# A fused diffusion layer on one core: which pieces of the first modulation's weights are split, and on which engine

## The chip, the cores and the metric

The kernel runs on one core of a Trainium2 chip. The metric is the device time of one execution in microseconds (us). Below, PE is the tensor engine (matrix products), DVE is VectorE, ACT is ScalarE, POOL is GpSimd and SP is the engine that issues most of the transfers. All data are 32 bit floats.

## What is computed

One layer of a diffusion backbone, on 128 context tokens and 512 latent tokens of width 1024. Two conditioning vectors (one for the context, one for the latent tokens) give shift, scale and gate for both halves of the layer:

```
mod_ctx = silu(c_ctx) @ w_mod + b_mod          # and mod_lat from c
sh1, sc1, gt1, sh2, sc2, gt2 = split(mod, 6)
h = rms_norm(x, gain0) * (1 + sc1) + sh1       # the "first modulation"
y = mixing(h)                                  # w_in, gated DeltaNet scans, short convolution, gates, w_out
x = x + gt1 * rms_norm(y, gain1)
h = rms_norm(x, gain2) * (1 + sc2) + sh2
y = (silu(gate) * up) @ w_ffn_out              # gate, up = split(h @ w_ffn_in, 2)
x = x + gt2 * rms_norm(y, gain3)
```

The mixing part has 8 heads with a chunked recurrent scan in two directions, whose state goes from chunk to chunk, and a short convolution branch `y_b = (bg * conv(cg * xs)) @ w_br_b`.

## The kernel before, in words

**Products in three parts.** A large product is made of three products of a faster number format (fp32r). `split` (L48) makes of a tile a high part, by a cast (L57), and a low part, by subtracting the high part from the tile (L58), each in two instructions of 512 columns: a "pair". By default the cast is on ScalarE and the subtraction on VectorE. `mm3` (L83 to L85) then multiplies high with high, high with low and low with high. `gemm_cm` (L87) does a whole gemm of 8 x 3 products of 320 columns into one PSUM bank `d`; the pool of these has three banks. A bank is free again when its reader has run: ScalarE's tanh L735, or VectorE's multiplications L716 and L724.

**The first modulation** (L762 to L856). Only sh1 and sc1 are needed before the layer's first gemm. Their weights come in two halves (`mods(0)`, `mods(1)`, each 512 of the 1024 channels), in each half for sc1 and sh1 four pieces `mr` of 128 x 2 x 512, so 16 pieces in all, loaded in that order. `mod_mm` (L782) multiplies a piece in one of two ways. A *direct* piece, named in the argument `direct`, goes in as it is, in 32 bit floats (L790, two products). A *split* piece is split first, into `msh` and `msl`, and has four fp32r products (L793 with the high part, L794 with the low part). `lows` and `highs` say on which engine the parts of piece 0, 1, 2, 3 are made: the low part of piece 3 on POOL, the others on VectorE; the high part of piece 2 on VectorE, the others on ScalarE. `mod_end` copies the product to a row `mrow` (L798) and turns it into a column by eight small products L180, copied out by L182. `scale_of` (L249) makes the scale s of sc1. `modulate(h)` then makes four of the eight blocks k of h: on ScalarE the high part hT0 (L811, context and latent columns apart), on VectorE the same in full precision over xT (L813) and the difference as low part hT1 (L815). The gemms of the layer, from L83 on, need these.

**The scans.** For each of four pairs of heads p, `scan(p)` (L599) goes through eight steps. A step has two sub-steps: products L643 with EW, then with KU, each into the PSUM tile s, and after each two copies into the state tile RS, one on ScalarE and one on VectorE (L647 after EW, L658 or L661 after KU). Each sub-step needs the copies of the one before. L673 makes the output products from what is there. Other work is there to fill the gaps: gemms of the gates, `gate_th` (tanh L735 into a tile gt), the short convolution, `short` (L701), and the steps of `row_job` (L185), which adds up the rows of the second modulation on VectorE, two L196 of 128 x 1024 for each weight tile; their sums go through L57/L58 (cph, cpl) and L208/L209 to a row.

**The short convolution.** `short(i)` multiplies two gemms into a tile cx (L710, L716), convolves it into cy (L717, then in `conv` L379, L381 and the two edges L384 and L386, of one column each), and multiplies cy with a third gemm, half by half (L724). cx, cy and the gates' gt take turns in two buffers of one tag, "dt".

**What sets the order.** In the first modulation the order on SP is written out. On the other engines a scheduler of the framework sets the order of all instructions of the program when it is built, from priorities (`high_priority`), the dependences and its own costs. So an edit at one place can change the order elsewhere. An engine runs its instructions in that order.

Of the kernel before, what the change touches and what calls it, by code (L numbers as in the profile page):

```python
# [21 lines left out]
CTX = 128  # L22
LAT = 512
TOK = CTX + LAT
# [13 lines left out]
class Kernel:  # L38
# [700 lines left out]
    def run(self):  # L739
        nc, tc, I, O = self.nc, self.tc, self.I, self.O  # L740
# [21 lines left out]
        with ExitStack() as st:  # L762
            xp = pool(st, "xp")
            psn = pool(st, "psn", 3, space=PSUM)
            psm = pool(st, "psm", 2, space=PSUM)
            ma = lambda: psm.tile([P, 512], F32, name="m", tag="m")
            pri = lambda n: tc.high_priority(offset=n)

            def mod_load(blk, h):
                row = xp.tile([5, 512], F32, name="mrow", tag="mrow", bufs=4)  # L770
                nc.gpsimd.dma_start(out=row[4:5, :], in_=I["b_mod"][blk, :, h * 512:(h + 1) * 512])
                raws = []
                for kk in range(KT // 2):
                    raw = xp.tile([P, 2, 512], F32, name="mr", tag="mr", bufs=9)
                    nc.sync.dma_start(out=raw, in_=I["w_mod1"][blk, h, kk])
                    raws.append(raw)
                return row, raws

            lows = (nc.vector, nc.vector, nc.vector, nc.gpsimd)
            highs = (nc.scalar.copy, nc.scalar.copy, nc.vector.tensor_copy, nc.scalar.copy)  # L780

            def mod_mm(raws, direct):  # L782

                ps = ma()
                for kk, raw in enumerate(raws):
                    sp = None if kk in direct else self.split(raw, [P, 2, 512], "ms", xp, 4, True, lows[kk], highs[kk])
                    for i in range(2):
                        k = 2 * kk + i
                        if sp is None:
                            nc.tensor.matmul(ps[0:4, :], lhsT=self.cz[:, k, :], rhs=raw[:, i],  # L790
                                             start=k == 0, stop=k == KT - 1)
                        else:
                            nc.tensor.matmul(ps[0:4, :], lhsT=self.cs[:, k, :], rhs=sp[0][:, i], start=k == 0, stop=False)  # L793
                            nc.tensor.matmul(ps[0:4, :], lhsT=self.cs[:, k, :], rhs=sp[1][:, i], start=False, stop=k == KT - 1)  # L794
                return ps

            def mod_end(h, out, ps, row):
                nc.scalar.copy(out=row[0:4, :], in_=ps[0:4, :])  # L798
                self.cm_finish(out, lambda: psn.tile([P, 512], F32, name="n", tag="n"))(h, row)

            def mods(h, loads, direct):
                prods = [mod_mm(loads[n][1], direct[n]) for n in range(2)]
                for n, name in enumerate(("sc1", "sh1")):
                    mod_end(h, cm[name], prods[n], loads[n][0])
                self.scale_of(cm["sc1"], 0, cm["s1"], slice(4 * h, 4 * h + 4))

            def modulate(h):
                s1 = cm["s1"]
                for k in range(4 * h, 4 * h + 4):
                    for v, s in ((0, slice(0, CTX)), (1, slice(CTX, TOK))):  # L810
                        nc.scalar.activation(out=hT[0][:, k, s], in_=xT[:, k, s], func=AF.Identity,  # L811
                                             scale=s1[:, k, v:v + 1], bias=cm["sh1"][:, k, v:v + 1])
                        nc.vector.tensor_scalar(out=xT[:, k, s], in0=xT[:, k, s], scalar1=s1[:, k, v:v + 1],  # L813
                                                scalar2=cm["sh1"][:, k, v:v + 1], op0=ALU.mult, op1=ALU.add)
                    nc.vector.tensor_tensor(out=hT[1][:, k, :], in0=xT[:, k, :], in1=hT[0][:, k, :].bitcast(F32),  # L815
                                            op=ALU.subtract)

            def norms():
                for t in range(NT):
                    r = self.rstd([xs[t]], xp, "n1")  # L820
                    nc.vector.tensor_scalar(out=xs[t], in0=xs[t], scalar1=r, scalar2=None, op0=ALU.mult)
                    for g in range(2):
                        ps = psn.tile([P, 512], F32, name="n", tag="n")
                        for i in range(4):
                            k = 4 * g + i
                            nc.tensor.transpose(ps[:, i * P:(i + 1) * P], xs[t][:, k * P:(k + 1) * P], self.ident)
                        nc.scalar.copy(out=xT[:, 4 * g:4 * g + 4, t * P:(t + 1) * P],
                                       in_=ps.rearrange("p (k x) -> p k x", x=P))

            xT = xp.tile([P, KT, TOK], F32, name="xT")  # L830
            with tc.manual_schedule(engines={mybir.EngineType.SP}):
                with pri(200000):
                    self.cond()
                    xs = []
                    for t in range(NT):
                        x = xp.tile([P, D], F32, name=f"x{t}")
                        nc.sync.dma_start(out=x, in_=xrow(t))
                        xs.append(x)
                    loads = [mod_load(blk, 0) for blk in (1, 0)]
                    self.constants()  # L840
                with pri(300000):
                    norms()
                with pri(150000):
                    mods(0, loads, ((0, 3), (0, 1)))
                with pri(150000):
                    if 1 == 0:
                        wg = self.load_w(I["w_in"][0], [P, KT, P])
                    loads = [mod_load(blk, 1) for blk in (1, 0)]
                    if 1 == 1:
                        wg = self.load_w(I["w_in"][0], [P, KT, P])  # L850
                with pri(150000):
                    modulate(0)
                with pri(150000):
                    mods(1, loads, ((0, 3), (0, 1)))
                with pri(300000):
                    modulate(1)  # L856
        self.dbg("hT", hT[0].bitcast(F32))
# [117 lines left out]
        for j in range(KT):  # L975
# [6 lines left out]
            for n, y in ((1, yb), (0, ya)):  # L982
                for h in range(2):
                    s = slice(h * HALF, (h + 1) * HALF)
# [203 lines left out]
        def first(j):  # L1188
            o = prepared[j]
            A, C = acc(), acc()  # L1190
            if j in saved:
                p1, u = saved[j]["p1"], tmp("u2")
                block(A, o["S2"], T2, True)
                with high():
                    add(u, p1, A)
            else:
                p1, u = tmp("p1"), None
                block(A, o["A11"], B11, True)
                with high():
                    nc.scalar.copy(out=p1, in_=A)  # L1200
            block(C, o["S1"], T1, True)
            return dict(o=o, A=A, C=C, p1=p1, u2=u)
# [41 lines left out]
        with tc.manual_schedule(engines={mybir.EngineType.PE}):  # L1244
            for step, *x in ((some, range(3), 0), (prod, 0, 1), (prod, 1, 1), (prod, 2, 1), (prod, 3, 0), (modulate, 0), (prod, 3, 1), (modulate, 1), (prod, 4, 0), (modulate, 2), (prod, 4, 1)):
                step(*x)
# [21 lines left out]
            for i, j in enumerate(rest):  # L1268
                if i + 1 < len(rest):
                    prepare(rest[i + 1], rest[i + 1] < EARLY)  # L1270
                v = first(j)
# [160 lines left out]
```

## Time and profile before

| | us |
|---|---|
| median of 3 runs | 1089.17 |
| lowest and highest | 1086.23, 1091.02 |
| the profiled execution | 1085.44 |
| its span, first to last instruction | 1083.7 |
| busy in it: PE, DVE | 1019.8, 836.9 |
| busy in it: ACT, POOL | 483.2, 141.9 |

The profile is of one execution. The times of its rows count from the start of its span. A busy PE is not PE at its peak, since products are pipelined and their ends are modelled: two gemm products of 0.31 us each start 0.15 us apart. "Granted clock" is the share of TensorE's full clock (2.4 GHz) that the chip granted in a stretch; 0.50 is 1.2 GHz. The mean over the span is 0.981.

### The profile page before, as it was taken

The page shows a single profiled execution, that of the slowest core. Times are in us where ns is not written, and L with a number is a line of the kernel's source. Part 1 is how long each engine was busy: PE and PEld are TensorE (multiplying, and loading weights), DVE is VectorE, ACT ScalarE, POOL GpSimd, SP SyncE. Part 2 cuts the span into 40 slices and gives each one's busy share as a digit, 9 for nine tenths or more (in the row PEclk, how much of TensorE's full clock was granted, in tenths as well). Part 3 has the DMA queues.
Part 4 walks back from the last instruction along what each step waited for, and adds up shares of the span by engine and source line. Part 5 has one row for each costly group of instructions (what it writes and reads, how often), then busy time and mean ns, then how long its engine had stood idle before and what let it go on. Part 6 is the DMA issues. An engine that isn't in the chain of part 4 may idle for free.

```text
span 1083.7 us, 19694 instructions
## 1 busy us (share of the span) xinstructions
PE 1019.8 (94%) x7729; PEld 925.9 (85%) x7729; DVE 836.9 (77%) x1698; ACT 483.2 (45%) x927; POOL 141.9 (13%) x168
## 2 busy tenths in 40 slices
PE   6999988988988989999998998999999999999997
PEld 3699987878887788899996887999999999788885
DVE  5767997897898888895895789888777775975336
ACT  5568436415525323434223476444445444624321
POOL 2215321153063050101000000000000000000000
PEclk9999989998999999999999998999999999999999
DMA  9335712163282374557853532323222322552214
GB/s 346 144 91 136 205 60 75 57 138 107 62 188 89 99 179 166 173 166 241 309 183 116 180 113 88 104 86 98 93 79 78 98 83 74 176 171 99 79 39 156
DMA packets 47399, 141.52 MB, mean 131 GB/s; under 512 B 9517, under 2 KB 10034, under 8 KB 47306
## 3 DMA queue, kind: packets, MB, share of 16 engines
q1 hardware_dynamic: 42746, 127.10, 35.9%
q0 software_dynamic: 4560, 13.15, 5.6%
q8 instruction: 61, 1.00, 0.4%
q14 instruction: 32, 0.26, 0.1%
HBM read 117.57 MB, written 12.18 MB: 120 GB/s over the span
## 4 chain that ended last, share of the span: by engine, by line
PE 63%; DVE 18%; DMA 3%; ACT 2%; issue 2%; SPq 1%; POOL 0%; DVEq 0%; ACTq 0%; POOLq 0%
PE acc L1166 21%; PE d L85 6%; PE d L83 6%; PE d L84 6%; PE acc L84 5%; PE acc L83 5%; PE acc L85 5%; PE d L1166 3%; DVE X L561 3%; DVE otmp L559 2%; PE s L643 2%; DVE wl L58 2%; PE v L614 1%; PE v L673 1%; DVE RT L565 1%
## 5 line engine op out<-in xcount | busy, mean ns | idle before, releaser
L83 PE MATMUL d<-hT,wh 128*128 128x320 f32 x720 | 228.4, 318 | 1.8 <-DVE cy L724 1.8
L85 PE MATMUL d<-hT,wl 128*128 128x320 f32 x720 | 228.9, 318 | 0.4 <-DVE wl L58 0.4
L84 PE MATMUL d<-hT,wh 128*128 128x320 f32 x720 | 227.2, 316 | 0.0
L57 ACT CAST wh<-wr 128x512 fp32r<-128x512 f32 x150 | 88.1, 620 | 155.1 <-PE d L84 90.4
L83 PEld LDWEIGHTS d<-hT,wh 128*128 128x128 f32 x720 | 137.3, 191 | 4.3 <-DVE cy L724 2.1
L85 PEld LDWEIGHTS d<-hT,wl 128*128 128x128 f32 x720 | 137.3, 191 | 4.2 <-issue 1.2
L84 PEld LDWEIGHTS d<-hT,wh 128*128 128x128 f32 x720 | 137.5, 191 | 2.0 <-issue 0.3
L58 DVE TENSOR_TENSOR wl<-wr,wh 128x512 fp32r<-128x512 f32 x150 | 103.1, 709 | 44.3 <-ACT wh L57 43.5
L1166 PE MATMUL acc<-mh,wl 128*128 128x320 f32 x280 | 86.9, 310 | 1.8 <-DVE wl L1101 1.8
L83 PE MATMUL acc<-wh,as 128*128 128x512 f32 x220 | 85.7, 390 | 2.1 <-ACT as L1300 2.1
L1166 PE MATMUL acc<-mh,wh 128*128 128x320 f32 x280 | 87.0, 311 | 0.3 <-ACT early L1180 0.3
L1166 PE MATMUL acc<-ml,wh 128*128 128x320 f32 x280 | 86.7, 310 | 0.0
L84 PE MATMUL acc<-wl,as 128*128 128x512 f32 x220 | 85.6, 389 | 0.0
L85 PE MATMUL acc<-wh,as 128*128 128x512 f32 x220 | 85.5, 389 | 0.0
L196 DVE SCALAR_TENSOR_TENSOR gacc<-wr,cv,gacc 128x1024 f32<-128x1024 f32 x64 | 80.7, 1280 | 4.0 <-DMA wr<-in_w_mod_dram 3.7
L1105 ACT CAST wh<-wr 128x512 fp32r<-128x512 f32 x66 | 40.7, 623 | 71.6 <-PE acc L1166 36.9
L1105 ACT CAST wh<-S 128x512 fp32r<-128x512 f32 x88 | 54.3, 621 | 36.3 <-PE d L1166 19.6
L1101 DVE TENSOR_TENSOR wl<-S,wh 128x512 fp32r<-128x512 f32 x88 | 60.2, 688 | 3.8 <-ACT wh L1105 2.9
L1101 DVE TENSOR_TENSOR wl<-wr,wh 128x512 fp32r<-128x512 f32 x66 | 45.4, 690 | 19.1 <-ACT wh L1105 18.1
L1166 PEld LDWEIGHTS acc<-mh,wl 128*128 128x128 f32 x280 | 52.8, 189 | 2.1 <-DVE wl L1101 2.0
L1166 PEld LDWEIGHTS acc<-mh,wh 128*128 128x128 f32 x280 | 52.7, 188 | 0.6 <-ACT early L1180 0.6
L1166 PEld LDWEIGHTS acc<-ml,wh 128*128 128x128 f32 x280 | 52.8, 189 | 0.0
(365 smaller groups left out, 2344.0 us busy)
## 6 DMA issues: line engine op xcount, KB each, us to landing
wr<-in_w_ffn_in_dram SPq DMA_DIRECT2D x48, 512.0 KB
wr<-in_w_in_dram SPq DMA_DIRECT2D x45, 512.0 KB
wr<-in_w_mod_dram SPq DMA_DIRECT2D x32, 512.0 KB
wr<-in_w_ffn_out_dram SPq DMA_DIRECT2D x22, 512.0 KB
mr<-in_w_mod_dram SPq DMA_DIRECT2D x16, 512.0 KB
thd<-gt SPq DMA_DIRECT2D x16, 320.0 KB
bth<-thd SPq DMA_DIRECT2D x16, 320.0 KB
wr<-in_w_br_dram SPq DMA_DIRECT2D x8, 512.0 KB
```

The costliest lines, as they stand in the source:

```text
L57: (high or nc.scalar.copy)(out=hi[:, s], in_=raw[:, s])
L58: (low or nc.vector).tensor_tensor(out=lo[:, s], in0=raw[:, s], in1=hi[:, s].bitcast(F32), op=ALU.subtract)
L83: mm(out, lhsT=ah, rhs=bh, start=start, stop=False)
L84: mm(out, lhsT=ah, rhs=bl, start=False, stop=False)
L85: mm(out, lhsT=al, rhs=bh, start=False, stop=stop)
L196: nc.vector.scalar_tensor_tensor(out=acc[v], in0=w, scalar=self.cv[:, k, v:v + 1], in1=acc[v], op0=ALU.mult, op1=ALU.add)
L559: nc.vector.tensor_tensor(out=t, in0=B[:, j + 1:32, j:j + 1].broadcast_to([P, n, j]), in1=X[:, j:j + 1, 0:j].broadcast_to([P, n, j]), op=A ...
L561: nc.vector.tensor_tensor(out=X[:, j + 1:32, 0:j], in0=X[:, j + 1:32, 0:j], in1=t, op=ALU.subtract)
L643: mm(ps[half(c2), o:o + 64], lhsT=w(d, c2, t, hd), rhs=R[:, d, c2, t, hd, :], start=True, stop=True)
L1101: tt = lambda o, a, b, op: nc.vector.tensor_tensor(out=o, in0=a, in1=b, op=op)
L1105: nc.scalar.copy(out=dst[0], in_=src)
L1166: nc.tensor.matmul(ps, lhsT=A[x][:, k], rhs=B[y][:, k], start=start and k == 0 and n == 0, stop=k == 3 and n == 2, skip_group_check=True)
```

## The change

All low parts of the modulation's pieces are made on VectorE. In the first half one piece of sc1 (piece 0) and one of sh1 (piece 0) stay direct, where two of each were. In the second half sc1 has none and sh1 has piece 3. So 3 of 16 pieces are direct where 8 were, and 13 are split. In `modulate` the two ScalarE instructions of a block come ahead of its two VectorE instructions, where they alternated. The edit adds a line, so line numbers behind L812 are higher by one after it.

```
--- before.py
+++ after.py
@@ -776,7 +776,7 @@
                     raws.append(raw)
                 return row, raws
 
-            lows = (nc.vector, nc.vector, nc.vector, nc.gpsimd)
+            lows = (nc.vector,) * 4
             highs = (nc.scalar.copy, nc.scalar.copy, nc.vector.tensor_copy, nc.scalar.copy)
 
             def mod_mm(raws, direct):
@@ -810,6 +810,7 @@
                     for v, s in ((0, slice(0, CTX)), (1, slice(CTX, TOK))):
                         nc.scalar.activation(out=hT[0][:, k, s], in_=xT[:, k, s], func=AF.Identity,
                                              scale=s1[:, k, v:v + 1], bias=cm["sh1"][:, k, v:v + 1])
+                    for v, s in ((0, slice(0, CTX)), (1, slice(CTX, TOK))):
                         nc.vector.tensor_scalar(out=xT[:, k, s], in0=xT[:, k, s], scalar1=s1[:, k, v:v + 1],
                                                 scalar2=cm["sh1"][:, k, v:v + 1], op0=ALU.mult, op1=ALU.add)
                     nc.vector.tensor_tensor(out=hT[1][:, k, :], in0=xT[:, k, :], in1=hT[0][:, k, :].bitcast(F32),
@@ -841,7 +842,7 @@
                 with pri(300000):
                     norms()
                 with pri(150000):
-                    mods(0, loads, ((0, 3), (0, 1)))
+                    mods(0, loads, ((0,), (0,)))
                 with pri(150000):
                     if 1 == 0:
                         wg = self.load_w(I["w_in"][0], [P, KT, P])
@@ -851,7 +852,7 @@
                 with pri(150000):
                     modulate(0)
                 with pri(150000):
-                    mods(1, loads, ((0, 3), (0, 1)))
+                    mods(1, loads, ((), (3,)))
                 with pri(300000):
                     modulate(1)
         self.dbg("hT", hT[0].bitcast(F32))
```

The change moves instructions on all engines, since the scheduler sets the order anew. Three places follow.

VectorE in the second half of the modulation, before: `msl` and `msh` are the low and high parts of pieces, `wl` that of the first gemm's weights, L813 and L815 belong to `modulate(0)`.

```order
L813 TENSOR_SCALAR xT<-xT,s_85,sh_81 128x512
L813 TENSOR_SCALAR xT<-xT,s_85,sh_81 128x128
L815 TENSOR_TENSOR hT_76<-xT,hT_75 128x640
L813 TENSOR_SCALAR xT<-xT,s_85,sh_81 128x512
L813 TENSOR_SCALAR xT<-xT,s_85,sh_81 128x128
L815 TENSOR_TENSOR hT_76<-xT,hT_75 128x640
L57 CAST msh<-mr 128x512 x2
L58 TENSOR_TENSOR msl<-mr,msh 128x512 x2
L813 TENSOR_SCALAR xT<-xT,s_85,sh_81 128x512
L815 TENSOR_TENSOR hT_76<-xT,hT_75 128x640
L249 SCALAR_TENSOR_TENSOR s_85<-sc_82,gains 128x8
L58 TENSOR_TENSOR wl<-wr,wh 128x512 x4
```

After, the same place (L814 and L816 are L813 and L815 of before):

```order
L814 TENSOR_SCALAR xT<-xT,s_85,sh_81 128x512
L58 TENSOR_TENSOR msl<-mr,msh 128x512 x2
L816 TENSOR_TENSOR hT_76<-xT,hT_75 128x640
L58 TENSOR_TENSOR msl<-mr,msh 128x512 x2
L57 CAST msh<-mr 128x512 x2
L58 TENSOR_TENSOR msl<-mr,msh 128x512 x2
L814 TENSOR_SCALAR xT<-xT,s_85,sh_81 128x128
L814 TENSOR_SCALAR xT<-xT,s_85,sh_81 128x512
L814 TENSOR_SCALAR xT<-xT,s_85,sh_81 128x128
L58 TENSOR_TENSOR wl<-wr,wh 128x512 x2
L816 TENSOR_TENSOR hT_76<-xT,hT_75 128x640
L58 TENSOR_TENSOR wl<-wr,wh 128x512 x2
```

Between the blocks of `modulate(0)` there stand now pairs of subtractions of pieces, in all seven pairs from the first block on, where there was one at this place.

PE in scan(3), the last one, before: one EW sub-step and the KU sub-step of the same step (tile s_4371), with products of a gate's gemm (bank d_5315).

```order
L643 MATMUL s_4371<-RS_3902,EW_534 64x64 x4
L83 MATMUL d_5315<-hT0_75,wh_5282 128x320
L84 MATMUL d_5315<-hT1_76,wh_5282 128x320
L85 MATMUL d_5315<-hT0_75,wl_5283 128x320
L83 MATMUL d_5315<-hT0_75,wh_5282 128x320
L84 MATMUL d_5315<-hT1_76,wh_5282 128x320
L85 MATMUL d_5315<-hT0_75,wl_5283 128x320
L83 MATMUL d_5315<-hT0_75,wh_5282 128x320
L84 MATMUL d_5315<-hT1_76,wh_5282 128x320
L643 MATMUL s_4371<-RS_3902,KU_3901 64x64 x4
L85 MATMUL d_5315<-hT0_75,wl_5283 128x320
L83 MATMUL d_5359<-hT0_75,wh_5352 128x320
```

After, from the KU sub-step of the step before that (tile s_4385 is s_4345 of before) on:

```order
L85 MATMUL d_5281<-hT0_75,wl_5249 128x320
L643 MATMUL s_4385<-RS_3942,KU_3941 64x64 x4
L643 MATMUL s_4398<-RS_3942,EW_574 64x64 x4
L673 MATMUL v_4457<-RS_3942,AQ_3943 64x64
L643 MATMUL s_4398<-RS_3942,KU_3941 64x64 x4
L643 MATMUL s_4411<-RS_3942,EW_574 64x64 x4
L643 MATMUL s_4411<-RS_3942,KU_3941 64x64 x4
L643 MATMUL s_4424<-RS_3942,EW_574 64x64 x4
L643 MATMUL s_4424<-RS_3942,KU_3941 64x64 x4
L673 MATMUL v_4457<-RS_3942,AQ_3943 64x64 x16
L643 MATMUL s_4437<-RS_3942,EW_574 64x64 x4
L643 MATMUL s_4437<-RS_3942,KU_3941 64x64 x4
```

The last gemm product is the first row here. From there on no gemm product stands between the sub-steps to the end of the scan; ten sub-steps follow each other, with output products L673 and row sums L208 and L209 between some.

VectorE around scan(3), before: the end of `short(1)` (tiles cx_5014 and cy_5015) ahead of the scan's first copy, which is the last row.

```order
L381 SCALAR_TENSOR_TENSOR cy_5015<-cx_5014,tapsc_163,cy_5015 128x10x63
L386 SCALAR_TENSOR_TENSOR cy_5015<-cx_5014,tapsc_163,cy_5015 128x1
L384 SCALAR_TENSOR_TENSOR cy_5015<-cx_5014,tapsc_163,cy_5015 128x1
L724 TENSOR_TENSOR cy_5015<-cy_5015,d_5141 128x320
L196 SCALAR_TENSOR_TENSOR gacc_4494<-wr_4564,cv_99,gacc_4494 128x1024
L196 SCALAR_TENSOR_TENSOR gacc_4495<-wr_4564,cv_99,gacc_4495 128x1024
L619 TENSOR_SCALAR EW_534<-v_4271 64x640 x2
L196 SCALAR_TENSOR_TENSOR gacc_4494<-wr_4568,cv_99,gacc_4494 128x1024
L724 TENSOR_TENSOR cy_5015<-cy_5015,d_5167 128x320
L647 COPY RS_3902<-s_4299 64x2x128
```

After, the end of the scan's copies (the same tiles are cx_5054 and cy_5055, bank d_5181 holds the half of short(1)'s third gemm):

```order
L661 COPY RS_3942<-s_4424 64x128
L196 SCALAR_TENSOR_TENSOR gacc_4534<-wr_5006,cv_99,gacc_4534 128x1024
L647 COPY RS_3942<-s_4437 64x128
L196 SCALAR_TENSOR_TENSOR gacc_4535<-wr_5006,cv_99,gacc_4535 128x1024
L661 COPY RS_3942<-s_4437 64x128
L58 TENSOR_TENSOR cpl_5013<-gacc_4534,cph_5012 128x512 x2
L647 COPY RS_3942<-s_4450 64x128
L386 SCALAR_TENSOR_TENSOR cy_5055<-cx_5054,tapsc_163,cy_5055 128x1
L724 TENSOR_TENSOR cy_5055<-cy_5055,d_5181 128x320
L58 TENSOR_TENSOR cpl_5031<-gacc_4535,cph_5030 128x512 x2
```

The edge L386 and the L724 of one half of cy stand now behind the scan's last copy, L647 of s_4450. The other edge and the other half stay ahead of the scan's second copy. On ScalarE the two L735 of gate_th(3), whose gt takes the buffer of cx_5054, stand behind the scan's last copy too.

## Rows read from the trace of the kernel before

**Rows 1.** The page's chain that ended last: shares of the span by engine.

```profile
PE 63%; DVE 18%; DMA 3%; ACT 2%; issue 2%; SPq 1%; POOL 0%; DVEq 0%; ACTq 0%; POOLq 0%
```

**Rows 2.** Stretches: length; busy us (instructions) of PE, PEld, DVE, ACT, POOL; PEclk; DMA share; GB/s.

```profile
30.00:42.00 12.00, 11.65 (x45) 4.00 (x43) 11.88 (x22) 7.48 (x16) 4.55 (x2) 1.00 0.33 134
434.00:455.00 21.00, 21.00 (x242) 17.47 (x241) 17.17 (x25) 8.20 (x21) 2.18 (x3) 1.00 0.61 195
455.00:566.00 111.00, 111.00 (x753) 109.82 (x752) 94.62 (x138) 37.79 (x66) 7.33 (x10) 1.00 0.66 223
566.00:580.00 14.00, 10.76 (x53) 8.58 (x53) 10.51 (x18) 4.78 (x8) 0.00 (x0) 0.93 0.00 1
```

**Rows 3.** Timeline of the modulation's second half: start, length, engine, line, operation, tiles, shape, count.

```profile
28.81 1.88 PE L790 MATMUL m<-mr,cz 128*4 128x512 f32 x4
...
31.91 4.49 ACT L811 ACTIVATE hT<-xT,sh,s 128x128 fp32r<-128x128 f32 x8
32.06 0.39 PE L793 MATMUL m<-msh,cs 128*4 128x512 f32 x1
...
32.29 0.40 PE L794 MATMUL m<-msl,cs 128*4 128x512 f32 x1
...
33.54 5.31 PE L790 MATMUL m<-mr,cz 128*4 128x512 f32 x12
...
34.60 0.80 DVE L813 TENSOR_SCALAR xT<-xT,s,sh 128x512 f32<-128x512 f32 x2
...
36.04 0.80 DVE L813 TENSOR_SCALAR xT<-xT,s,sh 128x512 f32<-128x512 f32 x2
...
37.45 4.57 POOL L58 TENSOR_TENSOR msl<-mr,msh 128x512 fp32r<-128x512 f32 x2 [11.22 <-ACT msh L57]
37.49 0.76 DVE L57 CAST msh<-mr 128x512 fp32r<-128x512 f32 x2
...
38.16 1.30 DVE L58 TENSOR_TENSOR msl<-mr,msh 128x512 fp32r<-128x512 f32 x2
...
42.07 0.39 PE L794 MATMUL m<-msl,cs 128*4 128x512 f32 x1 [0.42 <-POOL msl L58]
...
44.07 1.05 PE L180 MATMUL n<-selb,mrow 5*128 5x2 f32 x8
...
45.35 1.59 ACT L811 ACTIVATE hT<-xT,sh,s 128x128 fp32r<-128x128 f32 x3
```

**Rows 4.** Timeline in the last scan, same columns.

```profile
444.23 0.45 PE L643 MATMUL s<-RS,EW 128*64 128x64 f32 x8
...
444.73 0.26 ACT L647 COPY RS<-s 64x128 f32<-64x128 f32 x1 [0.90 <-PE s L643]
444.86 0.31 PE L83 MATMUL d<-hT,wh 128*128 128x320 f32 x1
...
445.01 0.31 PE L84 MATMUL d<-hT,wh 128*128 128x320 f32 x1
...
445.78 0.28 DVE L647 COPY RS<-s 64x128 f32<-64x128 f32 x1
...
445.99 1.27 DVE L196 SCALAR_TENSOR_TENSOR gacc<-wr,cv,gacc 128x1024 f32<-128x1024 f32 x1
...
447.36 0.28 DVE L661 COPY RS<-s 64x128 f32<-64x128 f32 x1
```

**Rows 5.** Stretches of 2 us in the second scan, columns as in rows 2.

```profile
380.00:382.00 2.00, 0.55 (x4) 0.28 (x2) 1.97 (x2) 0.00 (x0) 2.00 (x2) 1.00 0.00 0
...
384.00:386.00 2.00, 2.00 (x27) 1.88 (x24) 1.37 (x5) 0.70 (x1) 0.66 (x3) 0.50 0.49 95
386.00:388.00 2.00, 2.00 (x13) 2.00 (x12) 2.00 (x8) 0.44 (x1) 2.00 (x4) 0.77 0.69 139
```

**Rows 6.** Waits between 560 and 582 us: in total, times, longest.

```profile
PE d L209 <- DVE cpl L58: 1.6, 2, 0.8
...
PE acc L84 <- DVE wol L58: 1.1, 1, 1.1
```

More of the change, by code (lines that the diff above doesn't have):

```diff
@@ L777, in mod_load @@
                 return row, raws
-            lows = (nc.vector, nc.vector, nc.vector, nc.gpsimd)
+            lows = (nc.vector,) * 4
             highs = (nc.scalar.copy, nc.scalar.copy, nc.vector.tensor_copy, nc.scalar.copy)
@@ L812, in modulate @@
                                              scale=s1[:, k, v:v + 1], bias=cm["sh1"][:, k, v:v + 1])
+                    for v, s in ((0, slice(0, CTX)), (1, slice(CTX, TOK))):
                         nc.vector.tensor_scalar(out=xT[:, k, s], in0=xT[:, k, s], scalar1=s1[:, k, v:v + 1],
@@ L843, in run @@
                 with pri(150000):
-                    mods(0, loads, ((0, 3), (0, 1)))
+                    mods(0, loads, ((0,), (0,)))
                 with pri(150000):
@@ L853, in run @@
                 with pri(150000):
-                    mods(1, loads, ((0, 3), (0, 1)))
+                    mods(1, loads, ((), (3,)))
                 with pri(300000):
```

## The prediction

> **What bounds the kernel now.** I read the page's chain of waits first, then the table of stretches, then the timeline of two of them. The chain that ended last is 63% TensorE (PE) and 18% VectorE (DVE) [rows 1]. So time counts where PE is idle, or where something new makes it so. The stretches [rows 2] show three states. Before 45 us PE works for the modulation and feeds nobody at its full rate; VectorE is full from 30 to 42 us (11.88 of 12 us). From 434 to 566 us PE is busy without a gap (21.00 of 21.00, then 111.00 of 111.00), with VectorE at 82 and 85%: here each idle microsecond of PE is lost. From 566 to 580 us PE waits again (10.76 of 14.00). The forecast is made of the first stretch and of one place in the second, the last scan (433 to 455 us).
>
> **The change in the prologue.** A direct piece costs PE 1.77 us: three of them take 5.31 (33.54) [rows 3]. A split piece has four products 0.23 us apart (32.06 and 32.29), 0.92 us. Five pieces fewer direct are 5 x 0.85 = 4.2 us less PE work. Each split piece asks for a pair of casts (on ScalarE, or for the third piece of a product on VectorE, 0.76 at 37.49) and a pair of subtractions, 1.30 on VectorE (38.16) [rows 3]. VectorE had twelve subtractions, six pairs, and POOL four, two pairs; now VectorE has thirteen pairs. That is 7 x 1.30 = 9.1 us more on VectorE, three pairs of it in the first half of the modulation, where it has room, and four in the second, where it has none. POOL's pair at 37.45 took 4.57 us beside a busy VectorE, and the last product waited for it (42.07); that wait goes.
>
> *First half.* The shift is known, and modulate(0) starts, at 31.91 before [rows 3]. The four direct products of the next half in front of its row products (28.81, 1.88 us) go, of which 1.8 us is on the path, and one of its own pieces takes 0.85 less: 31.91 - 2.65 = about 29.3.
>
> *Second half.* By the order, VectorE now has this between that moment and the last subtraction of the shift: the first two steps of modulate, after ScalarE's two L811 that read the same xT (4.49 / 4 = 1.12 a k), so a start at 30.4; two k at 1.44 (34.60 to 36.04) = 2.9; two pairs of casts at 0.76 = 1.5; seven pairs of subtractions at 1.30 = 9.1. That ends at 30.4 + 13.5 = 43.9. The last direct piece follows on PE (0.23 + 1.77: 45.9), then nine gemm products 0.15 apart (444.86 and 445.01) [rows 4], behind which ScalarE's L798 hides, then L180 (44.07, 1.05): 48.3, and modulate(1) starts at 48.5 in place of 45.35. Two more gemm products than before are then done (nine against seven, 0.3 us). Sum: **+2.9**. Since PE is full from there, it isn't made up. Bounds: 0, if subtractions that I put behind 29.3 fit ahead of it; +5.5, if the clock falls and what stands behind 43.9 on PE (2.0 + 1.3 + 1.05) runs at half speed for some 2.5 us more. modulate's new order alone (two L811 ahead of two L814) costs nothing: each L814 waited for its L811 anyway, and ScalarE's 1.12 hides behind VectorE's 1.44.
>
> **The change in the last scan.** Nothing in the diff speaks of it, but the scheduler orders everything again. In the order before, eight to twelve gemm products stand between two sub-steps of the scan (L643). In the new one, from the KU part of the third step on, ten sub-steps stand with no gemm product between them. VectorE's order tells why: an edge of the short convolution (L386) and one half of the product with its third gemm (L724) moved behind the scan's last copy. So the tile cx, which L386 reads, stays held; the tanh that is to be written into its place (L735) stands behind the scan too; and the three PSUM banks of the gemms, one waiting for L724 and two for L735, stay taken. No further gemm can start.
>
> What does a sub-step cost then? PE's 0.45 us, then ScalarE's copy (0.26) and VectorE's (0.28), and on VectorE a row product L196 (1.27) stands between two copies. Two copies with a row product between and no wait are 445.78 and 447.36, 1.6 us apart [rows 4]. Nine such intervals leave PE 9 x (1.6 - 0.45) = 10.4 us. Off go 17 output products of 64 columns and four row sums of 512 that stay there; by the 0.15 of 320 columns these are 17 x 0.03 = 0.5 and 4 x 0.24 = 1.0: **+8.9**. Lower bound: the chain alone, 0.50 from L643 to the copy (444.23 to 444.73), 0.26 and 0.28, is 1.04: 9 x 0.59 - 1.5 = +3.8. That would want the row products elsewhere, and by the order they stand there, so I stay at the upper value. Upper bound: +10.4.
>
> *The clock.* No row shows PE this sparse at this place, but the second scan has its like: at 380 to 382 us PE was busy 0.55 of 2.00, and at 384 to 386 us the granted clock was 0.50 (1.2 GHz) with PE busy throughout, then 0.77 [rows 5]. That cost 2 x 0.50 + 2 x 0.23 = 1.5 us. The stretch here is sparse for 14 us, so I add **+1.5** once, when the gemms come back; bounds 0 and +3. Inside the stretch half speed costs little, as 0.9 + 0.26 + 0.28 still lies under 1.6.
> The Trainium skill, "TensorE: Matmul & The Clock Gate", section "HAM oscillation — how this bites in real kernels", says that each wait that idles the array long enough puts it back to half rate, so that the burst behind it starts cold, every time. By that rule the prologue's gaps would pay too, 2.5 more, and the sum would be +14.3. Before, the stretch 30 to 42 us has a clock of 1.00 [rows 2], so the sum goes without it.
>
> *Given back.* From 566 us on PE waits for VectorE, 1.6 us at L209 and 1.1 at L84 [rows 6]. If PE comes there some 10 us late and VectorE doesn't, they close: up to -2.7. But VectorE works through the same scan and its casts follow PE's freed buffers, so I take **-1.5**. Elsewhere the orders differ by small exchanges (0, within 2 either way), and late in the program they agree.
>
> **Sum.** 2.9 + 8.9 + 1.5 - 1.5 = +11.8 us. Against the profiled execution (1085.44, 3.7 below the median of the runs shown) that is 1097.2; against the median of 1089.17 it is **1101**.
>
> **The rivals.**
> *Faster: PE's path decides the prologue.* If the subtractions keep ahead of PE, the 4.2 us of direct products and the POOL wait (about 0.8) come off: modulate(1) at 40.3. That needs the last subtraction of the shift done by 38.6 and not at 43.9. For it: the lows of the first half have room. Against: VectorE was full already with four pairs fewer. It ends faster only if the last scan's idle PE is covered too, by waits further on; then -5: 1084. With the scan's loss at its floor it would be no change. Chance 0.08.
> *Only the prologue counts.* VectorE, at 85% behind the scan, may be what really ends that stretch (its row products and casts feed the waits at 566 us); work done early in the sparse stretch then spares it later, and most of the 8.9 is given back. For: the waits there are on VectorE. Against: PE never waits from 455 to 566 us. 2.9 + 0 to 3: 1092 to 1095 at the median. Chance 0.17.
> *The clock pays twice.* The clock falls in the thinned prologue and in the scan: 2.5 + 1.5 more and nothing given back (1.5): +17.3, 1106. For: the second scan's fall. Against: 1.00 from 30 to 42 us [rows 2], and PE has products to do in most of 29 to 44 us after the change. The rule of the Trainium skill named above ("TensorE: Matmul & The Clock Gate") would make this the expected case. Chance 0.13.
> *The change does nothing*, because POOL's subtractions were hidden: excluded for the work, which the order shows moved; what remains is in the second rival.
>
> **How the numbers follow.** The forecast (both losses, 1096 to 1104) has 0.62. The range runs from 1088, which takes in most of the second rival and the lower bounds of the scan, to 1107, the third rival; out are the first (0.08) and tails (about 0.1). A measurement of this kernel tells about 0.5%, 5.4 us, from no change. Slower than that: the forecast, the clock rival and a little of the second, 0.75. Within: most of the second and of the first at the scan's floor, 0.18. Faster: 0.07.
>
> **What would show it.** Right: the first L811 of modulate(1) at 48 to 49 us; no subtraction on POOL; in the last scan nine VectorE copies about 1.6 us apart, PE busy a third of those 14 us, no gemm product from the third step's KU part on; a granted clock near 0.5 right behind. Wrong in the prologue: modulate(1) at or before 45.35. Wrong in the scan: copies 1.1 us apart, or a stretch to 566 us that ends no later than before although the scan idled. If PE is full again at once and the time between the end of modulate(1) and 566 us is unchanged, the second rival holds.

## The result, and the profile after

The change makes the kernel slower: 1106.05 us (1103.12 to 1108.50, five runs) against 1089.17 us, a ratio of 1.0158, 95% interval 1.0135 to 1.0181. That is 17 us. The forecast was 1101, the range 1088 to 1107.

The profiled execution of the change took 1108.5 us, 2.5 more than its median, and that of before 3.7 less than its own, so the two traces lie 22.9 us apart in their spans (1106.6 and 1083.7). Sizes below are taken from ratios of medians where a run gives them, and from traces only place by place.

The page's chain that ended last, of the change, answers to [rows 1]:

```profile
PE 64%; DVE 22%; DMA 5%; ACT 4%; issue 3%; POOL 1%; SPq 0%; DVEq 0%; ACTq 0%; POOLq 0%
```

VectorE has 22% of it in place of 18, and DMA 5 in place of 3.

The stretches, with the columns of [rows 2]:

```profile
30.00:42.00 12.00, 9.09 (x33) 2.49 (x33) 10.52 (x20) 10.74 (x22) 0.00 (x0) 0.72 0.39 156
...
434.00:455.00 21.00, 14.84 (x174) 12.17 (x172) 19.16 (x27) 5.38 (x17) 0.00 (x0) 0.84 0.60 191
...
534.00:579.00 45.00, 43.31 (x285) 41.59 (x285) 38.03 (x58) 11.95 (x20) 0.00 (x0) 1.00 0.67 226
```

Three of these stretches differ from before. From 30 to 42 us PE is busy 9.09 us where it was 11.65, and its clock is 0.72 where it was 1.00. From 434 to 455 us it is busy 14.84 of 21 where it was busy throughout, at 0.84. And from 534 to 579 us, a stretch that before had no gap, 1.69 us are idle.

The end of the modulation, in the timeline of the change (answers to [rows 3]):

```profile
30.60 1.20 ACT L811 ACTIVATE hT<-xT,sh,s 128x128 fp32r<-128x128 f32 x2
31.12 0.35 DVE L814 TENSOR_SCALAR xT<-xT,s,sh 128x128 f32<-128x128 f32 x1 [2.85 <-ACT hT L811]
31.70 1.12 ACT L57 CAST msh<-mr 128x512 fp32r<-128x512 f32 x2
...
32.35 0.59 PE L793 MATMUL m<-msh,cs 128*4 128x512 f32 x1 [1.99 <-ACT msh L57]
...
43.10 1.28 DVE L58 TENSOR_TENSOR msl<-mr,msh 128x512 fp32r<-128x512 f32 x2
43.52 2.23 POOL L878 MEMSET EW<- 128x2560 f32 x1
...
43.83 0.39 PE L794 MATMUL m<-msl,cs 128*4 128x512 f32 x1 [0.55 <-DVE msl L58]
...
44.30 2.04 DVE L814 TENSOR_SCALAR xT<-xT,s,sh 128x128 f32<-128x128 f32 x3
...
44.76 1.88 PE L790 MATMUL m<-mr,cz 128*4 128x512 f32 x4
...
48.34 0.42 PE L84 MATMUL d<-hT,wh 128*128 128x320 f32 x1 [0.34 <-DVE hT L816]
...
48.84 1.05 PE L180 MATMUL n<-selb,mrow 5*128 5x2 f32 x8
...
50.12 1.20 ACT L811 ACTIVATE hT<-xT,sh,s 128x128 fp32r<-128x128 f32 x2
```

The shift of the first half is known at 30.6 (31.91 before). The first cast of a piece of the second half stands on ScalarE behind two L811, at 31.70, and PE waits 1.99 us for it. VectorE too stood idle ahead of its first L814 at 31.12, for 2.85 us. From 31.83 VectorE is full and PE waits for its subtractions, as at 43.83. The last direct piece follows at 44.76, the gemm products behind it wait for VectorE in turn (48.34), and modulate(1) starts at 50.12 in place of 45.35.

The last scan, in the same timeline (answers to [rows 4]):

```profile
442.38 0.29 DVE L661 COPY RS<-s 64x128 f32<-64x128 f32 x1 [0.48 <-ACT RS L661]
...
448.58 0.29 DVE L661 COPY RS<-s 64x128 f32<-64x128 f32 x1
448.90 1.28 DVE L196 SCALAR_TENSOR_TENSOR gacc<-wr,cv,gacc 128x1024 f32<-128x1024 f32 x1
...
448.92 0.69 PE L643 MATMUL s<-RS,EW 128*64 128x64 f32 x8 [0.95 <-DVE RS L661]
...
457.02 0.28 DVE L647 COPY RS<-s 64x128 f32<-64x128 f32 x1
...
457.23 0.20 DVE L386 SCALAR_TENSOR_TENSOR cy<-cx,tapsc,cy 128x1 f32<-128x1 f32 x1
...
457.47 0.49 DVE L724 TENSOR_TENSOR cy<-cy,d 128x320 f32<-128x320 f32 x1
```

From the copy at 442.38 to that at 457.02 there are nine intervals, 14.64 us, from 1.40 to 2.11 us and 1.63 on the mean. A row product L196 fills VectorE between two copies in most of them, and PE waits for the copy, 0.95 us in the row shown. In these 14.64 us PE is busy 7.86. The edge L386 and the half product L724, for which a PSUM bank and the buffer of cx are held, follow at 457.23 and 457.47; the next gemm product on hT starts at 460.73.

The clock in and behind that scan, columns as in [rows 5]:

```profile
448.00:450.00 2.00, 0.69 (x8) 0.51 (x8) 1.94 (x3) 0.52 (x2) 0.00 (x0) 0.50 0.51 180
...
458.00:460.00 2.00, 2.00 (x42) 1.97 (x38) 1.06 (x2) 1.60 (x4) 0.56 (x2) 0.50 0.66 242
```

It falls in the scan, to 0.50, and again as the gemms come back.

The waits behind the gates' gemms: VectorE's between 530 and 582 us, then PE's between 533 and 603 us (answers to [rows 6]):

```profile
DVE gacc L196 <- DMA wr<-in_w_mod_dram: 8.1, 5, 2.2
```

```profile
PE d L83 <- DVE bth L988: 1.6, 4, 0.6
PE d L209 <- DVE cpl L58: 1.6, 2, 0.8
PE acc L84 <- DVE wol L58: 1.2, 1, 1.2
```

PE's waits for cpl and wol at the stage's end stand nearly as before, 1.6 and 1.2 us for 1.6 and 1.1. New are the waits of a gemm for a PSUM bank that VectorE frees at L988. In one of them the whole chain can be read, on VectorE and then on PE:

```profile
538.38 1.28 DVE L196 SCALAR_TENSOR_TENSOR gacc<-wr,cv,gacc 128x1024 f32<-128x1024 f32 x1 [2.25 <-DMA wr<-in_w_mod_dram]
539.59 0.48 DVE L988 SCALAR_TENSOR_TENSOR bth<-bth,d 128x320 f32<-128x320 f32 x1
```

```profile
540.12 0.42 PE L83 MATMUL d<-yah,wh 128*128 128x320 f32 x1 [0.42 <-DVE bth L988]
```

A row product waits 2.25 us for its weights, L988 stands behind it on VectorE, and PE waits 0.42 us for the bank. In all VectorE's row products wait 8.1 us for weights.

### The profile page after: what moved, and what is told of

It is laid out like the page before. It is cut to its first block, busy times and chain, and to the rows that moved or that the text cites. A ratio compares the mean times of both kernels' runs of the same rounds, so it can differ in the third digit from the quotient of the medians.

```text
span 1106.6 us, 19726 instructions
## 1 busy us (share of the span) xinstructions
PE 1029.2 (93%) x7729; PEld 932.9 (84%) x7729; DVE 844.2 (76%) x1712; ACT 485.1 (44%) x935; POOL 139.8 (13%) x164
## 4 chain that ended last, share of the span: by engine, by line
PE 64%; DVE 22%; DMA 5%; ACT 4%; issue 3%; POOL 1%; SPq 0%; DVEq 0%; ACTq 0%; POOLq 0%
PE acc L1167 20%; PE d L83 7%; PE d L85 6%; PE d L84 6%; PE acc L84 5%; PE acc L85 5%; PE acc L83 5%; PE d L1167 3%; DVE otmp L559 3%; DVE X L561 3%; DVE wl L58 2%; DMA wr<-in_w_mod_dram 2%; PE s L643 2%; DVE gacc L196 1%; DMA wr<-in_w_ffn_in_dram 1%
## 5 line engine op out<-in xcount | busy, mean ns | idle before, releaser
L85 PE MATMUL d<-hT,wl 128*128 128x320 f32 x720 | 230.8, 321 | 0.0
L84 PE MATMUL d<-hT,wh 128*128 128x320 f32 x720 | 229.2, 319 | 0.3 <-DVE hT L816 0.3
L83 PEld LDWEIGHTS d<-hT,wh 128*128 128x128 f32 x720 | 139.0, 193 | 5.7 <-DVE cy L724 1.8
L85 PEld LDWEIGHTS d<-hT,wl 128*128 128x128 f32 x720 | 139.3, 194 | 2.8 <-issue 1.1
L84 PEld LDWEIGHTS d<-hT,wh 128*128 128x128 f32 x720 | 139.3, 193 | 1.9 <-DVE hT L816 0.6
L196 DVE SCALAR_TENSOR_TENSOR gacc<-wr,cv,gacc 128x1024 f32<-128x1024 f32 x64 | 80.3, 1279 | 11.3 <-DMA wr<-in_w_mod_dram 11.2
L84 PE MATMUL acc<-wl,as 128*128 128x512 f32 x220 | 85.6, 389 | 0.0
L85 PE MATMUL acc<-wh,as 128*128 128x512 f32 x220 | 85.5, 389 | 0.0
```

Source lines behind the costliest of these rows:

```text
L83: mm(out, lhsT=ah, rhs=bh, start=start, stop=False)
L84: mm(out, lhsT=ah, rhs=bl, start=False, stop=False)
L85: mm(out, lhsT=al, rhs=bh, start=False, stop=stop)
L196: nc.vector.scalar_tensor_tensor(out=acc[v], in0=w, scalar=self.cv[:, k, v:v + 1], in1=acc[v], op0=ALU.mult, op1=ALU.add)
```

## The experiments

Each ratio is against the kernel before on the same chip, with its 95% interval. What matters for each run is the order of instructions that the scheduler gave it behind the modulation: that of the kernel before, that of the change, or one of those named below. The new loop in `modulate` alone gives an order equal to that of before on PE, VectorE and ScalarE, instruction for instruction, and the change without that loop gives an order equal to the change's. So no run has that part alone; what remains are the pieces and the low parts.

**e1, the second half's pieces as before.** Its order behind the modulation is that of before.

```diff
-                    mods(1, loads, ((), (3,)))
+                    mods(1, loads, ((0, 3), (0, 1)))
```

> The change, but with the second half's pieces as before (10 split pieces in all, all low parts on VectorE). The order behind the modulation is here that of the kernel before, the last scan is filled. Theory (the loss is VectorE's full second half, +4 to +5 us, and the new order behind the modulation, +12 to +18): neither is here, POOL's slow subtractions are gone, so 1 to 3 us faster than before: 1086 to 1088. Rival (each split piece costs, wherever it stands): two of five extra pieces, so some 5 us or more slower, 1094 or above.

Measured: 1091.44 us, ratio 1.0024 (1.0008 to 1.0039), 2.6 us slower. Neither theory: too slow for mine, too fast for the rival. Without the change's order most of the 17 us are gone. But my reason for the prologue does not hold here: VectorE has only four pairs in the second half and modulate(1) starts at 48.38 all the same. ScalarE runs five L811 before the first cast of the second half; PE waits 1.66 us for it, to 32.97, and its clock is 0.59 and 0.56 from 34 to 38 us. From 37.11 on PE works without a gap, and VectorE's last subtraction has ended by 42.9: here PE's own work sets the start of modulate(1).

**e2, only the low parts moved.** Pieces as before; its order behind the modulation is that of the change.

```diff
-            lows = (nc.vector, nc.vector, nc.vector, nc.gpsimd)
+            lows = (nc.vector,) * 4
```

> Only the low parts moved to VectorE; 8 split pieces as before. The order behind the modulation is that of the change, with the last scan starved of gemm products. Theory: the prologue is no later than before, but the new order costs 12 to 18 us: 1099 to 1106, and from the last scan's start to its end PE is idle for some 6 us. Rival (the split pieces cost it all): within 3 us of before, 1086 to 1092.

Measured: 1100.31 us, ratio 1.0104 (1.0084 to 1.0124), 11.3 us slower by the ratio, a little under the 12 to 18 that I expected (the time lies within 1099 to 1106) and far from the rival. modulate(1) starts at 45.83, half a microsecond later than before, and in the last scan PE is idle 5.7 us:

```profile
425.00:450.00 25.00, 19.28 (x207) 14.94 (x205) 22.98 (x34) 6.14 (x20) 0.12 (x1) 0.74 0.58 178
```

So the greater part of the loss needs no further split piece: one word in a table of engines, and the order that follows from it, are enough. The change has 0.54% more, 5.9 us, for its five further pieces.

**e3, the change with an urgent convolution.**

```diff
-        nc.vector.tensor_scalar(out=y, in0=cx, scalar1=self.tapsc[:, 1, i:i + 1], scalar2=None, op0=ALU.mult)
-        self.conv(cx, self.tapsc, i, y, 0, 10, True)
+        with self.urgent():
+            nc.vector.tensor_scalar(out=y, in0=cx, scalar1=self.tapsc[:, 1, i:i + 1], scalar2=None, op0=ALU.mult)
+            self.conv(cx, self.tapsc, i, y, 0, 10, True)
```

> The change, with the short convolution on VectorE (L717 and the four instructions of conv) made urgent, so that the last scan has gemm products between its sub-steps again (144 in place of 73). Theory: the prologue's +4 to +5 stays, the last scan's loss of about 9 us goes: 1094 to 1098. Rival (all from the prologue): 1104 to 1108.

Measured: 1087.15 us, ratio 0.9992 (0.9977 to 1.0007). All of the loss is gone, more than the scan's share that I expected. The edit also orders instructions from some 236 us on anew, well ahead of the last scan, so this run doesn't tell the scan from the rest; e5 does.

**e4, the kernel before with the same edit,** its control.

> The kernel before with the same urgent convolution, as the control of the run above; the same order in scans 1 to 3 as there. Both theories: within 3 us of before (1086 to 1092), as there is no starved scan to mend. If it is 8 us faster the urgent convolution is a gain of its own and says nothing of the change.

Measured: 1087.34 us, ratio 0.9985 (0.9968 to 1.0002). No difference that can be told, as both theories had it, so the edit has no gain of its own on the kernel before. It is a control for what comes behind the first 250 us or so, since up to there its order differs from e3's.

**e5, the change with a third buffer for cx, cy and gt.** The order is the change's up to the last scan.

```diff
-        cx = ab.tile([P, TOK], F32, name="cx", tag="dt", bufs=2)
+        cx = ab.tile([P, TOK], F32, name="cx", tag="dt", bufs=3)
...
-        t = self.ab.tile([P, TOK], F32, name="gt", tag="dt", bufs=2)
+        t = self.ab.tile([P, TOK], F32, name="gt", tag="dt", bufs=3)
```

(and the same for cy)

> The change with three buffers of the tag dt in place of two; nothing else. The order of all engines is that of the change up to the last scan; there the tanh of the gate no longer waits for the convolution's tile, two PSUM banks come free, and 138 gemm products stand in the scan in place of 73. Theory (the starved last scan is the larger part of the loss): the 9 us of the scan, the clock behind it and the waits for the gates' tiles near 540 to 580 us go, 9 to 14 us: 1092 to 1097. Rival (the starved scan is made up for later, the earlier scans of the new order cost it): no more than 3 us go: 1103 to 1106.

Measured: 1092.20 us, ratio 1.0030 (1.0018 to 1.0043). From 1.0158 to 1.0030 are 1.3%, **13.9 us**, the upper end of what the theory gave. The last scan, the row of 434 to 455 us:

```profile
434.00:455.00 21.00, 20.84 (x241) 17.38 (x239) 17.57 (x28) 7.95 (x21) 0.44 (x1) 1.00 0.69 219
```

PE is busy 20.84 of 21 at a clock of 1.00. The starved scan, with what follows from it, is the larger part of the loss. e3 gained 4 us more than e5. In the traces that lies ahead of the starved place: from the 105th to the 553rd product L85 of the gemms on hT e3 takes 325.3 us and e5 331.7.

**e6, the kernel before with the third buffer,** whose order is that of before on PE, VectorE and ScalarE.

> The control: the kernel before with three buffers of dt. The order of no engine differs from that of before, the last scan was filled already. Both theories: within 2 us of before, 1086 to 1091. If it gains as much as the run above, the third buffer is a gain of its own.

Measured: 1086.20 us, ratio 0.9988 (0.9971 to 1.0006). The buffer gains nothing where the scan is filled.

**e7, e5 with fewer pairs in the second half.**

```diff
-                    mods(1, loads, ((), (3,)))
+                    mods(1, loads, ((0, 1), (3,)))
```

> The run with the third buffer, and in the second half of the modulation sc1 pieces 0 and 1 direct (11 split pieces in all): VectorE has five pairs of subtractions there in place of seven, PE 1.7 us more. Theory (VectorE's subtractions set the start of modulate(1)): two pairs are 2.6 us; modulate(1) starts at 47.0 to 48.0 us in place of 50, and the kernel is 2 to 3 us faster than the run with the third buffer alone. Rival (PE's own work or the clock set it): modulate(1) at 50 us or later, and no gain.

Measured: 1094.20 us, ratio 1.0047 (1.0030 to 1.0064): no faster than e5. The theory failed, and both signs of the rival came, modulate(1) at 50.07 us and no gain. The timeline says why:

```profile
30.96 4.47 ACT L811 ACTIVATE hT<-xT,sh,s 128x128 fp32r<-128x128 f32 x8
...
35.34 2.17 ACT L57 CAST msh<-mr 128x512 fp32r<-128x512 f32 x4
...
36.03 0.40 PE L793 MATMUL m<-msh,cs 128*4 128x512 f32 x1 [1.78 <-DVE msh L57]
36.22 2.50 DVE L58 TENSOR_TENSOR msl<-mr,msh 128x512 fp32r<-128x512 f32 x4
...
50.07 1.20 ACT L811 ACTIVATE hT<-xT,sh,s 128x128 fp32r<-128x128 f32 x2
```

With the first two pieces direct, all eight L811 of modulate(0) stand on ScalarE ahead of its first casts, which start at 35.34. On VectorE the cast of the first split piece stands behind L814 of modulate(0) too, and PE waits 1.78 us for it, to 36.03. VectorE's subtractions start at 36.22, where they began at 32.34 in the change. VectorE still ends its last pair by 44.0. What is later is PE: its clock falls behind the wait at 36.03, here the rows of 34 to 36 and 42 to 45 us:

```profile
34.00:36.00 2.00, 0.25 (x1) 0.00 (x0) 2.00 (x6) 2.00 (x5) 0.00 (x0) 1.00 0.16 57
...
42.00:45.00 3.00, 3.00 (x8) 0.88 (x9) 3.00 (x8) 1.20 (x3) 0.00 (x0) 0.50 0.00 0
```

PE is busy 0.25 of 2 us at 34 to 36, and works without a gap at 0.50 from 42 to 45 us on what stands ahead of modulate(1). So here PE's own work and its clock set the start, and not the number of pairs.

**e8, low parts on VectorE, 8 split pieces, urgent convolution.** The edits of e2 and e3; its order behind the modulation is that of e3.

> All low parts on VectorE, 8 split pieces as before, and the convolution urgent as in the run of the change with the filled scan, whose order it has behind the modulation. Theory (the prologue's delay is carried to the end one for one): modulate(1) starts at 45.8 in place of 49.5 us, so 3 to 4 us faster than that run: 1083 to 1085, and 4 us faster than before. Rival (the delay of the prologue is made up for where PE waits anyway, between 100 and 410 us): the same time as that run, 1086 to 1088.

Measured: 1082.94 us, ratio 0.9948 (0.9933 to 0.9964), a little below what the theory gave; the rival falls. It is 5.7 us faster than before and faster than both kernels of this case; e3, which differs in the five pieces and the loop alone, has 0.9992. The five pieces cost 0.44%, 4.8 us give or take 2.4, by this pair. The first L811 of modulate(1) in e8 (L812 there):

```profile
44.76 1.58 ACT L812 ACTIVATE hT<-xT,sh,s 128x128 fp32r<-128x128 f32 x3 [0.71 <-DVE s L249]
```

44.76 against 49.52 in e3, 4.8 us too. Why e8 gains over before was not tested; e9 below, with the low parts moved and without the urgent convolution, gains nothing, so the moved low parts alone are not the reason.

**e9, low parts on VectorE, 8 split pieces, third buffer.** The same question with the order of e5.

> Only the low parts on VectorE (8 split pieces as before), with the third buffer of dt: the order behind the modulation is that of the change with the third buffer, the last scan is filled. It differs from that run in the prologue alone. Theory (the five more split pieces delay the layer, one for one): modulate(1) starts at 45 to 46 us and the kernel is 3 to 4.5 us faster than the change with the third buffer, so within 2 us of before: ratio 0.998 to 1.000. Rival (the prologue is made up for; the rest of the loss lies in the new order of scans 0 to 2): the ratio stays at 1.003.

Measured: 1087.17 us, ratio 0.9996 (0.9982 to 1.0009), within the theory's span. e5 and e9 differ in the prologue alone, and modulate(1) starts at 48.33 and 45.18 (first the row of e5, then that of e9):

```profile
48.33 1.20 ACT L811 ACTIVATE hT<-xT,sh,s 128x128 fp32r<-128x128 f32 x2
```

```profile
45.18 1.21 ACT L811 ACTIVATE hT<-xT,sh,s 128x128 fp32r<-128x128 f32 x2 [0.72 <-DVE s L249]
```

3.2 us in the traces, 0.34% or 3.7 us (give or take 2) by the ratios. The rival, that the delay is made up for, falls. Against e2, which has e9's pieces and a starved scan, the third buffer gives 1.08%, 11.8 us.

Together: 13.9 us for the starved scan (the change against e5; 11.8 by e2 against e9), 3.7 for the five pieces (e5 against e9; 4.8 and 5.9 by the other two pairs), and nothing that can be told for moving POOL's low parts with all of the new order of scans 0 to 2 (e9 against before). Each figure has some 2 to 3 us either way. That they make 17 is no test, since each run of the chain is the next one's start; the other pairs are.

## Where the prediction was right, and where not

**The prologue, +2.9.** Right, somewhat small: 3.7 to 5.9 by three pairs of runs. The named sign, modulate(1) at 48 to 49 us, came in e5 (48.33), and not in the change's own trace (50.12) or in e3's (49.52), though all three have the same prologue, instruction for instruction. Two things part them. The direct products of PE that start at 17.74 before start at 19.01 in the change and at 17.96 in e5, so that 1 us stands ahead of every extra piece, and the shift came at 30.60 and 29.55 for the 29.3 that I had. And the nine gemm products of 0.15 us each took 2.3 us in the change, since VectorE gave them their operands late (48.34): its three L814 at 44.30 took 2.04 us beside POOL's L878. In e5 POOL's L878 came 0.9 us later than in the change, the three L814 took half as long, and the nine products took 1.5 us, as forecast:

```profile
43.25 1.06 DVE L814 TENSOR_SCALAR xT<-xT,s,sh 128x128 f32<-128x128 f32 x3
```

The sum for VectorE holds: 13.5 us were forecast, and from 31.12 to the end of its last pair, at 44.38, 13.3 passed. What I had not seen is that the casts of the second half stand behind modulate(0), ScalarE's behind L811 and in e7 also VectorE's behind L814. In e1 and e7, where VectorE has fewer pairs, PE waits 1.66 and 1.78 us for the first cast, its clock falls, and modulate(1) is no earlier than in e5. That the place of the casts is the reason is read from the traces; no run moved them alone.

**The last scan, +8.9, and its clock, +1.5.** Right, and somewhat large. Copies 1.63 us apart on the mean for 1.6; no gemm product among the sub-steps; the clock at 0.50 behind them. PE was busy 7.86 of 14.64 us, more than the third that I had named, in part at a clock of 0.50. I count in the traces the products L85 of the gemms on hT, 720 in each kernel (times in us):

| | 105th | 553rd | 720th | first L84 of w_out | 553rd to 720th | 720th to w_out |
|---|---|---|---|---|---|---|
| before | 96.7 | 427.1 | 515.2 | 578.3 | 88.1 | 63.1 |
| change | 101.6 | 437.2 | 534.1 | 600.6 | 96.9 | 66.5 |
| e2 | 97.3 | 430.0 | 527.2 | 594.8 | 97.2 | 67.6 |
| e5 | 99.8 | 431.5 | 519.7 | 583.0 | 88.2 | 63.3 |
| e9 | 96.7 | 425.6 | 513.8 | 576.8 | 88.2 | 63.0 |

The last scan lies between the 553rd and the 720th. With a starved scan that part takes 96.9 and 97.2 us, with a filled one 88.1 to 88.2: 8.8 to 9.1 us, the clock's fall included, against 10.4 forecast. At the 553rd product the change stands 5.7 us behind e5 already, though the order is the same up to there: its trace is of an execution 2.5 us above its median and e5's of one 1.2 below. So of these traces only such single parts are compared.

**What is given back, -1.5.** This step failed, and in its sign. I took the waits at 566 to 580 us [rows 6] for slack that a late PE would use up. They are not: they are a short chain at the end of a stage (cast, subtraction, product) whose cast starts when an earlier product of PE has ended. First before, then the change:

```profile
572.59 1.14 ACT L57 CAST cph<-gacc 128x512 fp32r<-128x512 f32 x2 [5.62 <-PE d L208]
```

```profile
594.96 1.14 ACT L57 CAST cph<-gacc 128x512 fp32r<-128x512 f32 x2 [5.67 <-PE d L208]
```

The chain moved with PE by 22 us, and its waits kept their length. In its place the part from the 720th product to w_out grew from 63.1 to 66.5 us: +3.4, and 67.6 in e2. There VectorE's row products wait for weights that are loaded late (8.1 us), L988 stands behind them though it is urgent, and PE waits for its bank (1.6 us; the rest of the +3.4 is not accounted for). e5 and e9, with a filled scan, have 63.3 and 63.0, so this too hangs on the starved scan. That SP's loads come later because the row products and gates of the last scan come in another order fits the waits; no run changed the loads alone, and it stays argued.

The two parts make 12.2 to 13.6 us in the traces, and the third buffer gave back 13.9, or 11.8 in e9 against e2.

**Elsewhere, 0.** One place was not small: behind the gemms' 105th product the change is 5.8 us slower than before in its trace (last section). But e9, with the change's order from there to the last scan, takes 328.9 us from the 105th to the 553rd product for 330.4 before, and its time is that of before: the new order as such costs nothing that can be told.

**The sum.** 1106.05 lies in the range and 2 us above the 1096 to 1104 that the forecast itself gave. Too little for the prologue and the wrong sign of what is given back were partly offset by too much for the scan, and that much is luck. "Only the prologue counts" is excluded, and so is the faster rival: VectorE did not keep ahead. Of the clock rival the fall in the prologue came true, behind the wait that ends at 32.35:

```profile
32.00:34.00 2.00, 1.51 (x4) 0.25 (x4) 2.00 (x4) 2.00 (x5) 0.00 (x0) 0.50 1.02 412
34.00:36.00 2.00, 1.80 (x5) 0.26 (x4) 2.00 (x5) 2.00 (x5) 0.00 (x0) 0.50 0.25 94
...
38.00:40.00 2.00, 1.45 (x6) 0.25 (x4) 2.00 (x5) 1.74 (x5) 0.00 (x0) 1.00 0.00 0
```

PE works there at 0.50, the lower of its two levels, 1.2 GHz. A wait with a burst at half rate behind it is what the Trainium skill, "TensorE: Matmul & The Clock Gate", section "HAM oscillation — how this bites in real kernels", describes, and the stretch 30 to 42 us at 0.72 agrees. The price of 2.5 us that the rival put on it is not seen: by 38 us the clock is back at 1.00, PE waits for VectorE again (0.57 us at 40.02, 0.55 at 43.83), and VectorE has had no gap since 31.83. That the rival gave just 1106 is chance; the waits for weights stand where it had the clock.

## What to carry to other kernels

Where a scheduler orders the whole program, an edit at its head can cost most far behind, as here some 400 us later. So compare the built orders before the times: a stretch that lives on filler work is worth a count of the filler. Filler needs free PSUM banks and tile buffers; one short instruction left behind a long chain can hold them, as L386 of 0.20 us, with L724 behind it, did here. A further buffer was a cheap guard: it gave back 13.9 us where the scan was starved, and neither gained nor cost anything that can be told where it was filled. And idle time at the end of a stage is slack only if what it waits for does not start from the engine that waits.

## What the runs showed of the hardware that was not expected

Which of VectorE and POOL pays when they work at once is not settled, in these traces, by which of them starts first. In the first preparation both multiply the same tile by rn, POOL 0.05 us ahead of VectorE. Before, POOL's product took 1.99 us and VectorE's 0.82, and PE waited 1.25 us for VectorE's:

```profile
102.33 1.99 POOL L449 TENSOR_TENSOR qh<-tk,rn 128x640 f32<-128x640 f32 x1 [5.67 <-DVE rn L438]
```

```profile
102.38 0.82 DVE L448 TENSOR_TENSOR kh<-tk,rn 128x640 f32<-128x640 f32 x1
...
103.34 0.74 PE L479 MATMUL w<-ident,kh 128*128 128x128 f32 x5 [1.25 <-DVE kh L448]
```

In the change POOL is again 0.05 us ahead, but its product took 1.26 us and VectorE's 1.89, and PE waited 2.80 us:

```profile
104.23 1.26 POOL L449 TENSOR_TENSOR qh<-tk,rn 128x640 f32<-128x640 f32 x1 [2.95 <-DVE fac L444]
```

```profile
104.28 1.89 DVE L448 TENSOR_TENSOR kh<-tk,rn 128x640 f32<-128x640 f32 x1
...
106.31 1.09 PE L479 MATMUL w<-ident,kh 128*128 128x128 f32 x4 [2.80 <-DVE kh L448]
```

Behind that wait PE's clock was 0.50 from 106 to 112 us; the first of the three rows:

```profile
106.00:108.00 2.00, 1.69 (x8) 1.72 (x9) 2.00 (x4) 0.00 (x0) 2.00 (x2) 0.50 0.00 0
```

POOL starts 0.05 us ahead in nine of the eleven traces, and there are two outcomes with nothing between: VectorE 0.82 and POOL 1.99 us in before, e1, e3, e4 and e9, VectorE 1.89 and POOL 1.26 in the change, e2, e5 and e8. So one engine takes its short time and the other is held. e5 and e9 have the same order of instructions there and differ, so the order does not settle it either. Between the 105th and the 121st product of the gemms this place took 9.7 us before and 15.5 in the change; with the order of the change it took 14.3 in e2, e5 and e8, where VectorE was held, and 12.2 in e3 and e9, where POOL was. What decides which of the two is held, no run here tells; spans on POOL are rough in these profiles.
